# One more batch through the DMA crossbar, and one load issued beside the crossbar transposes (RWKV time mixing, 16 x 2048 x 256)

## The chip, the cores and the metric

One core of a Trainium2 chip runs the whole problem. The metric is the device time of one execution in microseconds, the median of several runs; three runs of the kernel before gave 198.86 to 199.21, median 199.1. A profile of one execution gives, for every engine, when each instruction ran and what it waited for.

The engines are TensorE (PE, matrix products and its own transposes), VectorE (DVE), ScalarE (ACT), GpSimd (POOL) and SyncE (SP, which here only issues DMAs). Sixteen DMA engines move data between HBM and the on-chip memory SBUF; they serve a queue q1 (issued by SP: stores and crossbar transposes) and a queue q0 (issued by POOL: loads that turn float32 into bfloat16 on the way).

## The reference

```python
x_prev = np.zeros_like(x)
x_prev[:, 1:, :] = x[:, :-1, :].copy()
xk = x * time_mix_k + x_prev * (1 - time_mix_k)
xv = x * time_mix_v + x_prev * (1 - time_mix_v)
xr = x * time_mix_r + x_prev * (1 - time_mix_r)
k = xk.reshape(-1, d_model) @ key_weight
v = xv.reshape(-1, d_model) @ value_weight
r = xr.reshape(-1, d_model) @ receptance_weight
r_sigmoid = 1.0 / (1.0 + np.exp(-r))
wkv = v
out = (r_sigmoid * wkv).reshape(-1, d_model) @ output_weight
```

x is 16 batches of 2048 tokens of 256 channels, float32. The result depends on r and v only; k isn't used. So per token: mix it with the token before in two ways, two products with 256 x 256 matrices, a sigmoid, an elementwise product, and one more product.

## The kernel before, in words

**Units.** The tokens are worked through in 64 units of 512, four to a batch; the main loop runs over the unit number g. Channels must lie on the partitions for the products, so each batch is needed transposed (`xt`). For a unit, TensorE makes the r product (`psum_r`, four matmuls), the v product (`psum_v`, four) and the output product of an earlier unit (`psum_o`, eight small ones). ACT makes the sigmoid `s_sb` and copies the output to `o_sb`; DVE multiplies `s_sb` with `psum_v` into `z_sb`. The mixed input `mix` is made ahead of the unit in two steps: one half of the channels is scaled on POOL (`scale_pool`, line 364), the other on DVE (`scale`, 354) or ACT (`scale_act`, 638), and then DVE adds the shifted tokens (`add`, 376). From unit 10 on the scalings are made once for a pair of units, for r (m = 0) in one unit and for v (m = 1) in the next, and from `FREE` on the one for v on ACT.

**Two ways to transpose.** Batches 0 to 9 are loaded into SBUF tiles `x_bf` and transposed on TensorE (`transposes`, line 272: eight 128 x 128 transposes in a unit, for the unit six ahead), and ACT copies the result out of PSUM (289). Batches from `STAGED` = 10 on are loaded as bfloat16 into a DRAM tile `x_natural` instead, and one DMA from SP (`by_dma`, line 254) reads it through the crossbar, transposed, into `xt_both`: batches 10 to 12 in one instruction issued in unit 27, 13 to 15 in another in unit 39 (`T_AT`). Each waits until the last load of its group has landed (`after`); the loads of batches 12 and 15 are in two halves (`HALVED`). A few rows of zeros stand ahead of each batch in DRAM (`zero_rows`, one small DMA in each unit from 12 on), which give the token before the first.

**What sets the order.** The order of every engine's instructions is the program's order, and each engine and each queue takes its instructions one after another. POOL issues the loads between its scalings. Loads 13, 14 and 15 are issued in units 33, 34 and 35 (`STAGE_AT`), and a dependency (`tc.add_manual_dep`) makes each wait until the crossbar transpose before them (`last_t`) has landed. SP issues the stores and the crossbar transposes: ahead of a transpose, stores that are held back until the first half of the last load has landed (`FIRST`), then the transpose, then the stores that were kept meanwhile (`WAITING`). A store is for a pair of units and named by its second one; store 19 is that of units 18 and 19.

**Tiles for the output.** Seven `o_sb` tiles go round; from the pair number `SPARE` on, four of each eleven are taken from the `x_bf` tiles that no load needs any more.

Of the kernel before, what the change touches and what calls it, by code (L numbers as in the profile page):

```python
# [9 lines left out]
BF16 = mybir.dt.bfloat16  # L10
# [5 lines left out]
def kernel(  # L16
# [27 lines left out]
    B, S, D = x.shape  # L44
    P = 128
    KO = D // P
    J = S // P
    UJ = 4
    TU = UJ * P
    UB = J // UJ  # L50
# [2 lines left out]
    BYUNIT = 2  # L53
    LONG = 2
    H = UJ // 2
    STAGED = 10
    BYDMA = NU - STAGED * UB
    CROSS = NU - BYDMA - LOOK
    FREE = CROSS
    LATE_O = CROSS - 2  # L60
    T_AT = {27: 10, 39: 13}
    FIRST = {19: 27, 21: 27, 27: 39}
    WAITING = {23: 27, 25: 27, 29: 39, 31: 39, 33: 39, 35: 39}
    ZEROS_AT = 12
    SINGLE = NU - 6
    STAGED_PAIRS = range(STAGED, B - 1)
    STAGE_AT = {33: 13, 34: 14, 35: 15}
    GROUPS = [(2, 3), (4, 5, 6), (7, 8, 9), (10, 11, 12), (13, 14, 15)]
    HALVED = (12, 15)
    PAD = 16  # L70
    SPARE = 9 * UB // 2
    NX, NO = 4, 7
    START_T = [1, 3, 5, 6, 7, 9, 11, 12]
    AHEAD = 6
# [7 lines left out]
        (2, 0): (5,),  # L82
        (3, 0): (6,),
        (4, 0): (7,),
        (5, 0): (8, 10),
        (6, 0): (9,),
        (7, 0): (11,),
        (7, 1): (12,),
    }

    consts = ctx.enter_context(tc.tile_pool(name="consts", bufs=1))
    xpool = ctx.enter_context(tc.tile_pool(name="xpool", bufs=NX))
    dpool = ctx.enter_context(tc.tile_pool(name="dpool", bufs=2, space=bass.MemoryType.DRAM))
    xtpool = ctx.enter_context(tc.tile_pool(name="xtpool", bufs=2))
    mixpool = ctx.enter_context(tc.tile_pool(name="mixpool", bufs=3))
    zpool = ctx.enter_context(tc.tile_pool(name="zpool", bufs=3))
# [15 lines left out]
    loads = {}  # L112
    xt_both = {}
    xt = {}
# [32 lines left out]
    def load(b):  # L147
        if b < STAGED:
            x_bf[b] = xpool.tile([P, J, D], BF16, name="x_bf")
# [41 lines left out]
    for e in (2, 3):  # L191
        op = nc.gpsimd.dma_start(out=x_first[:, e - 2], in_=unit_rows(x, 0, e)[:, 0])  # L192
# [17 lines left out]
    def new_xt(b):  # L210
        if b >= BYUNIT:
            for group in GROUPS:
                if b != group[0]:
                    continue
                if b >= STAGED:
                    t = xtpool.tile([P, KO, len(group) * (PAD + S)], BF16, name="xt_both")
                    for k in range(len(group)):
                        xt[b + k] = t[:, :, k * (PAD + S) + PAD - 1 : (k + 1) * (PAD + S)]
                    xt_both[b] = t
                    return  # L220
                xt_both[b] = xtpool.tile([P, J + 1, KO, len(group), P], BF16, name="xt_both")
                for k in range(len(group)):
                    xt[b + k] = xt_both[b][:, :, :, k]
                    nc.gpsimd.memset(xt[b + k][:, 0, :, 0:1], 0.0)
            return
        xt[b] = consts.tile([P, UB * (UJ + 1), KO, P], BF16, name=f"xt_first{b}")
        (nc.vector if b == 0 else nc.gpsimd).memset(xt[b][:, 0, :, 0:1], 0.0)

    new_xt(0)
# [21 lines left out]
    def by_dma(b, after):  # L251

        new_xt(b)
        op = nc.sync.dma_start_transpose(
            out=xt_both[b], in_=x_both[b].rearrange("b s d -> (b s) d")
        )
        tc.add_manual_dep(op.ins, after.ins.name, SYNC, reason="not beside a load")
        return op
# [66 lines left out]
    def tokens(piece, off, ko=None):  # L325

        b, _, lo, hi = piece
        if b in STAGED_PAIRS:
# [3 lines left out]
            return cols if ko is None else cols[:, ko]  # L332
        if b < STAGED:
            cols = xt[b][:, slots(piece, off)]
# [227 lines left out]

    pads = [p for group in GROUPS if group[0] >= STAGED for p in new_staged(group)]
    tnext = 1
# [57 lines left out]
    for u in range(2, NU):  # L622
# [3 lines left out]
        for m, (b, _, lo, hi) in enumerate(pieces(u)):  # L626
            w = first[u][m]
            group = (b, m, lo, hi + TU if paired else hi)
# [17 lines left out]
    for g in range(NU - 1):  # L646
        ps_r = ps_r_pool.tile([P, KO, TU], FP32, name="psum_r")
        if g == 0:
            project_unmixed(ps_r, 0)
            advance(1)  # L650
            project_unmixed(ps_r, 1)
            wrap_slots(pieces(1)[0])
            scale(pieces(1)[0])
            last = add(pieces(1)[0])
        else:
            project(ps_r, g, 0)
        s_sb = zpool.tile([P, KO, TU], BF16, name="s_sb")
        nc.scalar.activation(out=s_sb, in_=ps_r, func=ACT.Sigmoid)  # L658
        advance(START_T[g] if g < len(START_T) else g + LOOK)
        if g in T_AT:  # L660
            half, whole = loads[T_AT[g] + 2]
            for pair in firsts.pop(g):
                store(nc.sync, *pair, after=half)
            last_t = by_dma(T_AT[g], whole)
            for pair in kept.pop(g, []):
                store(nc.sync, *pair)
        if LATE_O < g < NU - 2:
            output(g - 2, z_prev2)
        for p in products.get(g + 1, []):
            if g >= FREE and p[0][1] == 1:  # L670
                scale_act(p[0], (0,))
        for p in [q for q, _ in products[g]] + pooled[g]:
            last_unit_of = p[3] // TU - 1
            need = last_unit_of if p[0] < BYUNIT else min(last_unit_of + 1, UB - 1)
            assert UB * p[0] + need < tnext, (g, p, tnext)
            if g > AHEAD or p not in pooled[g]:
                wrap_slots(p)
        if g == 1:
            load(2)
            scale_act(pieces(2)[1], (1,))  # L680
        for p, kos in products[g]:
            if not (g - 1 >= FREE and p[1] == 1):
                scale(p, kos)
        for p in sums[g]:
            last = add(p)
        for p in pooled[g]:
            if p[0] >= BYUNIT:
                wrap_slots(p)
        ps_v = ps_v_pool.tile([P, KO, TU], FP32, name="psum_v")
        project(ps_v, g, 1)  # L690
        if g == 0:
            scale_act(pieces(1)[1], (0,))
            advance(2)
        z_sb = zpool.tile([P, KO, TU], BF16, name="z_sb")
        n = TU // 2 if g == NU - 2 else TU
        for c in range(0, TU, n):
            nc.vector.tensor_tensor(  # L697
                out=z_sb[:, :, c : c + n],
                in0=s_sb[:, :, c : c + n],
                in1=ps_v[:, :, c : c + n],  # L700
                op=ALU.mult,
            )
        for p in pooled[g]:
            wrap_slots(p, after=last)
            scale_pool(p, last)
        if ZEROS_AT <= g < ZEROS_AT + len(pads):
            zero_rows(*pads[g - ZEROS_AT])
        if g in STAGE_AT:
            b = STAGE_AT[g]
            loads[b] = load(b)  # L710
            for op in loads[b] if b in HALVED else [loads[b]]:
                tc.add_manual_dep(op.ins, last_t.ins.name, SYNC, reason="not beside transposes")
        for p in held[g]:
            add(p)
        if z_prev is not None and not LATE_O <= g < NU - 3:
            output(g - 1, z_prev)
        z_prev2, z_prev = z_prev, z_sb
# [31 lines left out]
```

## Time and profile before

| what | value |
|---|---|
| median of three runs | 199.1 us (198.86 to 199.21) |
| span of the profiled execution, first to last instruction | 197.1 us |
| the profiled execution's own time | the page gives its span only; the median of the runs is 2.0 above it |
| busy: PE / DVE / ACT / POOL | 97% / 93% / 90% / 44% |
| DMA queues q1 / q0, share of 16 engines | 60.3% / 41.6% |
| a unit with TensorE transposes / without | about 3.05 / 2.60 us |
| issue of the two crossbar transposes | 95.4 and 133.9 us |

In the rows, `L272` is line 272 of the kernel, `x32` a count, and times are in us unless said. `PE psum_r L384` is the r product, `psum_v L384` the v product, `psum_o L416` the output product, `ps_t L272` a TensorE transpose. In the rows by window the columns are the stretch and its length, busy time and instructions of PE, weight loads, DVE, ACT and POOL, the granted TensorE clock, the busy share of the DMA engines and GB/s. A row of a DMA queue gives packets, MB and the share of the time of 16 engines that the packets took; shares above 100% mean that packets of one engine overlap.

### The profile page before, as it was taken

What the parts mean: (1) busy time and instruction counts of PE and PEld (TensorE: products, weight loads), DVE (VectorE), ACT (ScalarE), POOL (GpSimd) and SP (SyncE); (2) the same over time, 40 slices, a digit from 0 to 9 for tenths busy, and PEclk for the clock granted to TensorE, in tenths of its full rate; (3) what the DMA queues carried; (4) which work ended last, traced back from release to release, by engine and by line L of the source; (5) the groups of instructions that cost most, each with busy time, mean ns of one, the idle gap of its engine ahead of it and who ended that gap; (6) DMA issues with size and microseconds to landing.
All of it is one profiled execution on the core that took longest, in us unless ns stands there. A gap on an engine that the chain in (4) does not pass through costs nothing.

```text
span 197.1 us, 3735 instructions
## 1 busy us (share of the span) xinstructions
PE 191.5 (97%) x1358; PEld 123.0 (62%) x1364; DVE 183.1 (93%) x286; ACT 177.1 (90%) x197; POOL 86.3 (44%) x117
## 2 busy tenths in 40 slices
PE   8999999999999999999999999999999999999992
PEld 3556676666666666666666666666666666666660
DVE  0999999999999999999999999999999999999962
ACT  3699899999999999999999999999999999999982
POOL 2845542443665635624334266444433444444200
PEclk9999999999999999999999999999999999999998
DMA  5999999999999999999999999999999999999985
GB/s 185 238 176 224 218 254 262 247 259 262 296 413 283 283 296 332 283 238 198 376 209 290 335 346 186 212 218 241 290 290 419 419 421 419 416 416 421 382 327 221
DMA packets 35593, 58.13 MB, mean 295 GB/s; under 512 B 26004, under 2 KB 27128, under 8 KB 30840
## 3 DMA queue, kind: packets, MB, share of 16 engines
q1 hardware_dynamic: 31792, 41.34, 60.3%
q0 software_dynamic: 3632, 16.44, 41.6%
q8 instruction: 10, 0.16, 0.3%
q10 hardware_dynamic: 152, 0.13, 0.2%
q14 instruction: 7, 0.06, 0.1%
HBM read 34.34 MB, written 39.90 MB: 377 GB/s over the span
## 4 chain that ended last, share of the span: by engine, by line
PE 90%; DMA 6%; POOL 1%; issue 0%; SPq 0%; ACT 0%
PE psum_r L384 27%; PE psum_v L384 27%; PE psum_o L416 27%; PE ps_t L272 8%; DMA x_bf<-in_x_dram 4%; DMA w_f<-n_receptance_weight_dram 2%; PE ps_t L416 1%; POOL x_bf L192 1%; SPq L174 0%; POOL wo_bf L195 0%; PE psum_v L416 0%; POOL x_bf L152 0%; PE ps_t L384 0%; PE psum_r L416 0%; ACT x_bf L446 0%
## 5 line engine op out<-in xcount | busy, mean ns | idle before, releaser
L364 POOL TENSOR_SCALAR mix<-xt_both,c_sb 128x1024 bf16<-128x1024 bf16 (+1 forms) x55 | 61.1, 1110 | 85.5 <-DVE mix L376 82.3
L697 DVE TENSOR_TENSOR z_sb<-s_sb,psum_v 128x1024 bf16<-128x1024 bf16 (+1 forms) x64 | 76.8, 1201 | 2.3 <-PE psum_v L384 1.1
L376 DVE TENSOR_TENSOR mix<-mix,xt_both 128x1024 bf16<-128x1024 bf16 x112 | 76.8, 696 | 1.4
L384 PEld LDWEIGHTS <-w_bf 128*128 128x128 bf16 x512 | 48.5, 98 | 39.2 <-DVE mix L376 0.8
L658 ACT ACTIVATE s_sb<-psum_r 128x1024 bf16<-128x1024 f32 x63 | 65.2, 1034 | 6.2 <-PE psum_r L384 6.0
L384 PE MATMUL psum_v<-mix,w_bf 128*128 128x512 bf16 (+1 forms) x252 | 64.8, 378 | 0.4 <-DVE mix L376 0.2
L384 PE MATMUL psum_r<-mix,w_bf 128*128 128x512 bf16 x250 | 64.6, 379 | 0.2
L416 PE MATMUL psum_o<-wo_bf,z_sb 128*128 128x256 bf16 x486 | 63.2, 273 | 0.0
L416 PEld LDWEIGHTS <-z_sb 128*128 128x128 bf16 x512 | 52.0, 103 | 17.9 <-DVE z_sb L510 0.7
L471 ACT COPY o_sb<-psum_o 128x1024 f32<-128x1024 f32 x50 | 51.2, 1023 | 5.0 <-PE psum_o L416 4.8
L289 ACT COPY xt_both<-ps_t 128x1024 bf16<-128x1024 bf16 x32 | 32.9, 1039 | 0.0
L272 PEld LDWEIGHTS <-x_bf 128*128 128x128 bf16 x304 | 19.8, 98 | 8.4 <-DMA x_bf<-in_x_dram 0.4
L272 PE MATMUL ps_t<-ident,x_bf 128*128 128x128 bf16 x304 | 22.7, 219 | 0.2 <-DMA x_bf<-in_x_dram 0.2
L354 DVE TENSOR_SCALAR mix<-xt_both,c_sb 128x1024 bf16<-128x1024 bf16 (+1 forms) x47 | 21.3, 463 | 0.0
L638 ACT ACTIVATE mix<-xt_both,c_sb 128x1024 bf16<-128x1024 bf16 x14 | 16.3, 1163 | 0.0
L376 DVE TENSOR_TENSOR mix<-mix,xt_first 128x1024 bf16<-128x1024 bf16 x15 | 10.5, 708 | 0.1
L471 ACT COPY x_bf<-psum_o 128x1024 f32<-128x1024 f32 x10 | 10.2, 1015 | 0.0
L354 DVE TENSOR_SCALAR mix<-xt_first,c_sb 128x512 bf16<-128x512 bf16 x22 | 6.6, 350 | 0.3 <-ACT xt_first L282 0.2
L289 ACT COPY xt_first<-ps_t 128x1024 bf16<-128x1024 bf16 x6 | 6.0, 1022 | 0.0
L557 POOL COPY xt_first<-xt_first 128x254 bf16<-128x254 bf16 x5 | 2.0, 392 | 7.2 <-DVE mix L376 7.2
L162 POOL DMA_DIRECT2D x_bf<-in_x_dram x8 | 4.7, 584 | 0.0
L364 POOL TENSOR_SCALAR mix<-xt_first,c_sb 128x512 bf16<-128x512 bf16 x6 | 4.1, 685 | 1.3 <-DVE mix L376 0.8
(68 smaller groups left out, 52.3 us busy)
## 6 DMA issues: line engine op xcount, KB each, us to landing
out_dram<-o_sb SPq DMA_DIRECT2D x25, 1024.0 KB, 12.1
x_bf<-in_x_dram POOLq DMA_DIRECT2D x8, 1024.0 KB, 15.8
x_natural<-in_x_dram POOLq DMA_DIRECT2D x4, 1024.0 KB, 11.8
out_dram<-x_bf SPq DMA_DIRECT2D x4, 1024.0 KB, 14.4
x_natural<-in_x_dram POOLq DMA_DIRECT2D x4, 512.0 KB, 12.7
out_dram<-x_bf SPq DMA_DIRECT2D x4, 512.0 KB, 4.7
x_bf<-in_x_dram POOLq DMA_DIRECT2D x6, 256.0 KB, 7.0
o_sb<-in_x_dram SPq DMA_DIRECT2D x4, 256.0 KB, 3.9
```

Source lines behind the costliest of these rows:

```text
L162: return nc.gpsimd.dma_start(out=x_bf[b], in_=rows(b), max_dma_last_dim=run)
L272: nc.tensor.transpose(out=ps[:, jj], in_=src[:, jj, ko * P : (ko + 1) * P], identity=idn)
L289: nc.scalar.copy(out=xt[b][:, j0 : j0 + UJ], in_=ps)
L354: nc.vector.tensor_scalar(out=mixed(piece, ko), in0=tokens(piece, 0, ko), scalar1=c_sb[:, m, ko : ko + 1], scalar2=None, op0=ALU.mult,)
L364: op = nc.gpsimd.tensor_scalar(out=mixed(piece, 1), in0=tokens(piece, 0, 1), scalar1=c_sb[:, m, 1:2], scalar2=1.0, op0=ALU.mult, op1=ALU.mult,
L376: return nc.vector.tensor_tensor(out=mixed(piece), in0=mixed(piece), in1=tokens(piece, 1), op=ALU.add)
L384: nc.tensor.matmul(out=ps[:, mo, :], lhsT=w_bf[:, m, ko, mo * P : (mo + 1) * P], rhs=mixed((b, m, e * TU + lo, e * TU + hi), ko), start=(k ...
L416: nc.tensor.matmul(out=ps[:, j, :], lhsT=slot[:, ko, j], rhs=wo_bf[:, ko, :], start=(ko == 0), stop=(ko == KO - 1),)
L471: nc.scalar.copy(out=o[:, j0 : j0 + UJ, :], in_=ps)
L638: nc.scalar.activation(out=mixed(piece, ko), in_=tokens(piece, 0, ko), func=ACT.Copy, scale=c_sb[:, m, ko : ko + 1],)
L658: nc.scalar.activation(out=s_sb, in_=ps_r, func=ACT.Sigmoid)
L697: nc.vector.tensor_tensor(out=z_sb[:, :, c : c + n], in0=s_sb[:, :, c : c + n], in1=ps_v[:, :, c : c + n], op=ALU.mult,)
```

## The change

Batch 9 goes by DRAM and the crossbar as well (`STAGED` = 9), as a group of its own, with its own crossbar instruction issued in unit 27 right ahead of that of batches 10 to 12; its transposed tile takes the place of batch 0's. The TensorE transposes end four units earlier, and what follows from their end (`FREE`, `LATE_O`, `SPARE`) moves with it. Load 9 is issued with load 8 and load 10 in the place that load 9 had. Load 13 is issued in unit 27 instead of 33 and no longer waits for the crossbar (`BESIDE`). Loads 14 and 15 stay in units 34 and 35 and still wait for `last_t`, which is the transpose of 10 to 12. Store 21 moves from ahead of the transposes to behind them.

```diff
-    STAGED = 10
+    STAGED = 9
-    T_AT = {27: 10, 39: 13}
-    FIRST = {19: 27, 21: 27, 27: 39}
-    WAITING = {23: 27, 25: 27, 29: 39, 31: 39, 33: 39, 35: 39}
+    T_AT = {27: (9, 10), 39: (13,)}
+    FIRST = {19: 27, 27: 39}
+    WAITING = {21: 27, 23: 27, 25: 27, 29: 39, 31: 39, 33: 39, 35: 39}
...
-    STAGE_AT = {33: 13, 34: 14, 35: 15}
-    GROUPS = [(2, 3), (4, 5, 6), (7, 8, 9), (10, 11, 12), (13, 14, 15)]
+    STAGE_AT = {27: 13, 34: 14, 35: 15}
+    BESIDE = (13,)
+    GROUPS = [(2, 3), (4, 5, 6), (7, 8), (9,), (10, 11, 12), (13, 14, 15)]
...
-    SPARE = 9 * UB // 2
+    SPARE = STAGED * UB // 2 - 2
...
-        (5, 0): (8, 10),
-        (6, 0): (9,),
+        (5, 0): (8, 9),
+        (6, 0): (10,),
...
-    dpool = ctx.enter_context(tc.tile_pool(name="dpool", bufs=2, space=bass.MemoryType.DRAM))
+    dpool = ctx.enter_context(tc.tile_pool(name="dpool", bufs=3, space=bass.MemoryType.DRAM))
+    firstpool = ctx.enter_context(tc.tile_pool(name="firstpool", bufs=1))
...
-                    t = xtpool.tile([P, KO, len(group) * (PAD + S)], BF16, name="xt_both")
+                    pool, name = (firstpool, "xt_first0") if len(group) == 1 else (xtpool, "xt_both")
+                    t = pool.tile([P, KO, len(group) * (PAD + S)], BF16, name=name)
...
-        xt[b] = consts.tile([P, UB * (UJ + 1), KO, P], BF16, name=f"xt_first{b}")
+        xt[b] = firstpool.tile([P, UB * (UJ + 1), KO, P], BF16, name=f"xt_first{b}")
...
-            half, whole = loads[T_AT[g] + 2]
+            half, whole = loads[T_AT[g][-1] + 2]
             for pair in firsts.pop(g):
                 store(nc.sync, *pair, after=half)
-            last_t = by_dma(T_AT[g], whole)
+            for b in T_AT[g]:
+                last_t = by_dma(b, whole)
...
-            for op in loads[b] if b in HALVED else [loads[b]]:
+            for op in () if b in BESIDE else loads[b] if b in HALVED else [loads[b]]:
                 tc.add_manual_dep(op.ins, last_t.ins.name, SYNC, reason="not beside transposes")
```

## The prediction

> **What bounds the kernel now.** I read the busy shares and DMA queues first, then the chain of waits, the windows, and the order of time of GpSimd (POOL), VectorE (DVE) and the SP queue around 95 to 125 us.
>
> ```profile
> span 197.1 us, 3735 instructions
> ...
> PE 191.5 (97%) x1358; PEld 123.0 (62%) x1364; DVE 183.1 (93%) x286; ACT 177.1 (90%) x197; POOL 86.3 (44%) x117
> ...
> q1 hardware_dynamic: 31792, 41.34, 60.3%
> q0 software_dynamic: 3632, 16.44, 41.6%
> ```
>
> TensorE is 97% busy, and the two DMA queues that matter (q1 the stores and crossbar transposes, q0 the loads) fill 60.3 + 41.6 = 101.9% of the 16 engines. So both are nearly full, and the chain says what a unit costs:
>
> ```profile
> 104.83 0.86 PE psum_r L384 x4
> 105.69 0.45 PE ps_t L272 x8
> ...
> 107.88 0.86 PE psum_r L384 x4
> ...
> 118.36 0.86 PE psum_r L384 x4
> ...
> 120.96 0.86 PE psum_r L384 x4
> ```
>
> Unit 31 starts at 104.83 and unit 32 at 107.88: 3.05 us with eight transposes in it (0.45). Units 36 and 37 start at 118.36 and 120.96: 2.60 us, without. A unit that loses its eight transposes is 3.05 - 2.60 = 0.45 shorter. (Unit numbers follow from counting back from the last unit, 63.)
>
> ```profile
> 160.00:165.00 5.00, 4.95 (x32) 3.22 (x32) 4.98 (x8) 4.59 (x6) 2.24 (x2) 1.00 1.01 419
> ```
>
> In the later stage PE (4.95 of 5) and DVE (4.98 of 5) are both full at a granted clock of 1.00, and the DMA engines too (share 1.01, 419 GB/s of stores). What is lost there once isn't caught up again.
>
> **The change, part by part.** *Removed:* batch 9's 32 TensorE transposes, done beside units 30 to 33: 4 x 0.45 = **1.8 us off the PE chain**. With them go four ACT copies and one DVE copy of the shifted column; two scalings of 0.46 us move from DVE to ACT because FREE falls from 34 to 30.
>
> ```profile
> L289 ACT COPY xt_both<-ps_t 128x1024 bf16<-128x1024 bf16 x32 | 32.9, 1039 | 0.0
> ...
> L354 DVE TENSOR_SCALAR mix<-xt_both,c_sb 128x1024 bf16<-128x1024 bf16 (+1 forms) x47 | 21.3, 463 | 0.0
> ...
> L638 ACT ACTIVATE mix<-xt_both,c_sb 128x1024 bf16<-128x1024 bf16 x14 | 16.3, 1163 | 0.0
> ...
> L142 POOL DMA_DIRECT2D x_natural<-zeros x6 | 3.3, 554 | 0.0
> ```
>
> ACT gives up 4 x 1.04 and takes 2 x 1.16, so it is relieved. Units 30 to 33 then look like units 34 and later, where DVE keeps PE's pace; I see nothing that withholds the 1.8. The seventh zero fill costs POOL 0.55 us at unit 18; POOL is busy 44% and it costs nothing there. Loads 9 and 10 change places on the queue with the same bytes, so load 12 should land when it does now. The output tiles keep their distance: two more sit in the old x tiles from unit 32 on, and a tile filled late is still reused only eleven tiles later; nothing.
>
> *Added to the DMA:* one crossbar batch, 2064 x 256 x 2 bytes = 1.057 MB.
>
> ```profile
> 138.00:148.00 10.00, 9.89 (x61) 6.24 (x62) 9.98 (x15) 9.18 (x10) 4.09 (x5) 1.00 1.27 290
> ```
> ```profile
> q0 software_dynamic: 352, 2.11, 102.4%
> ```
>
> Crossbar traffic alone runs at 290 GB/s (first row), so one batch is 1.057 / 0.290 = 3.64 us. From 120 to 130 us only loads ran: 2.11 MB landed, so one batch load (1.05 MB in bf16) takes 5.0 us of all engines. A store of 1.05 MB at 419 GB/s takes 2.5 us.
>
> *Moved:* load 13 to unit 27, without its wait for the crossbar.
>
> ```profile
> 95.09 1.12 POOL L364 TENSOR_SCALAR mix<-xt_both,c_sb 128x1024 bf16<-128x1024 bf16 x1 [2.12 <-DVE mix L376]
> 97.84 1.12 POOL L364 TENSOR_SCALAR mix<-xt_both,c_sb 128x1024 bf16<-128x1024 bf16 x1 [1.63 <-DVE mix L376]
> ```
> ```profile
> q0 software_dynamic: 12, 0.10, 55.6%
> ```
>
> It is issued at about 96.2, in a gap of 1.63 us on POOL, so the 0.56 us issue is free. Its packets come some 2 us later, near 98.3, beside the transposes: the second row is the load queue from 116.5 to 117.5 us, with the first 12 packets of the load that is issued at 114.71 now. Store 21 moves behind them: 2.5 us of traffic less ahead, on the same SP queue; store 19 stays ahead.
>
> *What then waits:* loads 14 and 15 still depend on the last crossbar transpose (of 10 to 12), and load 14 is still issued by POOL in unit 34. This is the step I count most carefully.
>
> ```profile
> 113.48 1.12 POOL L364 TENSOR_SCALAR mix<-xt_both,c_sb 128x1024 bf16<-128x1024 bf16 x1 [2.33 <-DVE mix L376]
> 114.71 0.56 POOL L162 DMA_DIRECT2D x_natural<-in_x_dram  x1
> 116.23 1.11 POOL L364 TENSOR_SCALAR mix<-xt_both,c_sb 128x1024 bf16<-128x1024 bf16 x1 [0.96 <-DVE mix L376]
> 117.30 0.55 POOL L162 DMA_DIRECT2D x_natural<-in_x_dram  x1
> 118.66 1.11 POOL L364 TENSOR_SCALAR mix<-xt_both,c_sb 128x1024 bf16<-128x1024 bf16 x1 [0.81 <-DVE mix L376]
> 119.72 1.10 POOL L158 DMA_DIRECT2D x_natural<-in_x_dram  x2
> 121.41 1.11 POOL L364 TENSOR_SCALAR mix<-xt_both,c_sb 128x1024 bf16<-128x1024 bf16 x1 [0.58 <-DVE mix L376]
> ```
> ```profile
> L162 POOLq EVENT_SEMAPHORE x9: 17/17/43, 17.6 to 114.2; - x9
> ```
> ```profile
> L254 SPq DMA_TRANSPOSE xt_both<-x_natural x2: 12865/14030/15195, 95.4 to 133.9; - x2
> ...
> DMA to landing us min/median/max: 15.7/17.3/18.8
> ```
>
> The first transpose was issued at 95.4 and landed 18.8 later, at 114.2; the last wait of the POOL queue for a load ends at just that time, and POOL's scaling ran to 114.6 anyway. So the wait stands in POOL's own stream and is free today by 0.4 us. After the change, POOL reaches load 14 when scaling 34 ends: 116.23 + 1.11 - 1.8 = 115.5. If the crossbar lands at T, later than that, POOL stands still, and behind it stand scaling 35, the two halves of load 15, and scaling 36: 0.1 + 0.56 + 1.06 + 1.10 + 1.12 + 0.1 = 4.05 us of POOL work until scaling 36 is done, at T + 4.05.
>
> ```profile
> 122.36 1.30 DVE L376 TENSOR_TENSOR mix<-mix,xt_both 128x1024 bf16<-128x1024 bf16 x2
> 123.66 1.22 DVE L697 TENSOR_TENSOR z_sb<-s_sb,psum_v 128x1024 bf16<-128x1024 bf16 x1
> ```
>
> DVE wants it in the second of these two adds, which starts some 0.6 in, at 122.97 today, 121.2 after. So DVE is late by T - 117.1; behind the add stands unit 37's product z, which frees psum_v for unit 38.
>
> ```profile
> 122.69 0.86 PE psum_v L384 x4
> ...
> 125.29 0.86 PE psum_v L384 x4
> ```
>
> z ends at 124.88, PE wants the bank at 125.29: 0.41 with the handover, of which 0.2 stays after the following, longer DVE unit. **PE's loss is T - 117.3, and the whole gain is gone at T = 119.1.**
>
> ```profile
> q0 software_dynamic: 180, 1.34, 80.3%
> q1 hardware_dynamic: 110, 0.75, 23.1%
> ```
>
> *T.* The transposes wait for load 12, so they start at 95.4 as now. The nearest row is the second transpose, which also had one store in front of it: 15.7 from issue to landing (of which 3 x 3.64 = 10.9 is traffic). 95.4 + 15.7 + 3.64 for batch 9 = 114.7 without the load. What load 13 adds is shown nowhere. Lower end 0: the crossbar leaves 419 - 290 = 129 GB/s unused. Upper end 5.0: by the records the engines are 127% busy with the crossbar alone, and where loads and stores overlap (the two rows above, 80 to 88 us) their shares only add up, to 103%. A crossbar that fills the engines' time with small packets is nearer to these two rows, so I take 5.0 less some 0.5 that the load finds in the slow start of the transposes: **T = 114.7 + 4.5 = 119.2**. The Trainium skill, "DMA: Bandwidth & Descriptors", "Queues, rings and completion order", says that each DMA engine takes turns between its queues packet by packet. No run here shows a load beside a transpose; by that rule the load's whole 5.0 would go on top, T = 119.7, and by the spare rate it would be 114.7. The first transpose's 18.8, less 2.5 for the missing store, would give 0.6 more; and a second transpose instruction may pay a start of its own. So T lies in 114.7 to 121.
>
> *Sum:* -1.8 + (119.2 - 117.3 = 1.9) = +0.1. The sum is made in the profiled span of 197.1; the page gives nothing of what lies around it, and the runs' median is 2.0 above, which I keep: 199.1 + 0.1 = **199.2**.
>
> *The end.* DMA gets 3.64 more to do. Today 95.4 to 133.9 holds 35.2 us of traffic (three crossbar batches 10.9, three loads 15.0, two stores behind the first transpose and most of two ahead, 9.3) in 38.5; after it is 38.8 (3.64 more), and with the load beside the start some 2 less idle: the second transposes start about 2.0 later, and the stores behind them too.
>
> ```profile
> 186.00:196.00 10.00, 7.35 (x52) 4.72 (x50) 5.61 (x10) 6.62 (x12) 0.00 (x0) 0.98 0.78 306
> ```
>
> The last 10 us hold 2.2 us of idle DMA, so this is covered, barely, when PE ends no earlier; with the full PE gain it would take about 0.2 of it back. Batch 13 itself is wanted by POOL at unit 49, some 2 us after it would land.
>
> ```profile
> 134.00:138.00 4.00, 4.00 (x27) 2.70 (x26) 3.98 (x7) 3.59 (x5) 2.13 (x2) 1.00 1.16 197
> ```
>
> **Rivals.** *The load finds room* (T up to 117.3): for it the 129 GB/s; against it the 127%. POOL's wait then ends before it matters: 199.1 - 1.8 + 0.2 (the end, above) = 197.5; with half of the load hidden (114.7 + 2.5 = 117.2) the same. *Slower: POOL's queue behind load 14.* The same wait decides, from T = 119.5 on (0.2% over): with the second instruction's start exposed (the row above: the first four us of the old second one move 197 of 290 GB/s, some 1.3 to 2 us lost) T = 121.0, PE loses 3.7, 199.1 - 1.8 + 3.7 = 201.0. For it: two instructions where one was; against it: the load can fill that gap. *The change isn't felt*: batch 9 lands late, and unit 36 waits as long as it gained, 199.1; against it, 95.4 + 15.7 - 2 x 3.64 + 5.0 = 108.8 is the latest for one batch, and POOL wants it at about 112.
>
> **How the numbers follow.** A difference of 0.2% (0.4 us) is about what a measurement can tell. Main case, T near 119.2 (118.5 to 120.5: 198.5 to 200.5): 0.45, of which 0.08 faster, 0.25 same, 0.12 slower. Room for the load: 0.32, faster. Long POOL wait: 0.18, slower. Not felt: 0.05, same. So faster 0.40, same 0.30, slower 0.30. The range is 197.4 (full gain, a little taken back by the end) to 201.0 (T = 121); the main case alone is 198.5 to 200.5.
>
> **What would show it.** Units 30 to 33 at 2.60 apart. The landing of the transpose of 10 to 12, near 119.2, as the end of POOL's wait ahead of load 14; POOL idle before it from 115.5, scaling 36 near 122.2, and a hole of about 1.9 us in PE's chain at unit 38. DMA share about 1 through the load. If the transpose lands by 117.3 there is no hole and I am wrong on the faster side; if after 120.5, on the slower.

## The result, and the profile after

The changed kernel takes 216.6 us in the median of four executions (211.4, 214.4, 218.7, 227.7); the kernel before takes 199.2 beside it (198.9 to 199.6). The ratio is 1.068, interval 1.062 to 1.074: slower, and far outside the predicted 197.4 to 201.0; the shortest execution is still 12 us longer than the kernel before. The ratio leaves out the two longest executions as disturbed, while the profile is of the one of 218.7, so the sizes read from it are those of a longer execution.

The page of the changed kernel, its span and engines, its two large queues, and the shares of the chain that ended last:

```profile
span 216.9 us, 3671 instructions
...
PE 192.8 (89%) x1324; PEld 122.1 (56%) x1332; DVE 183.4 (85%) x283; ACT 175.4 (81%) x195; POOL 87.7 (40%) x117
...
q1 hardware_dynamic: 35952, 42.40, 65.0%
q0 software_dynamic: 3664, 16.44, 39.2%
...
PE 71%; DMA 22%; POOL 1%; issue 1%; DVE 1%; SPq 0%; ACT 0%; POOLq 0%
```

TensorE was 97% busy and is 89% now. The chain was PE's alone around the first transposes; now 22% of it is DMA (6% before), and 18 of the 22 are two pieces (the chain in order of time: start, length, what):

```profile
95.48 17.55 DMA xt_first<-x_natural
113.03 21.51 DMA xt_both<-x_natural
```

The first is the crossbar of batch 9 as far as the issue of the second instruction; the second is that of batches 10 to 12, which lands at 113.03 + 21.51 = 134.5. The prediction had 119.2. SP's queue and then POOL in order of time (start, length, instruction, and in brackets the idle time before it and what ended it) show who stood still:

```profile
95.48 17.25 SPq L257 DMA_TRANSPOSE xt_first<-x_natural  x1
113.03 19.46 SPq L257 DMA_TRANSPOSE xt_both<-x_natural  x1
...
153.32 13.54 SPq L257 DMA_TRANSPOSE xt_both<-x_natural  x1
```
```profile
96.18 0.56 POOL L164 DMA_DIRECT2D x_natural<-in_x_dram  x1
...
122.58 2.93 POOL L367 TENSOR_SCALAR mix<-xt_first,c_sb 128x1024 bf16<-128x1024 bf16 x2 [12.22 <-DMA xt_first<-x_natural]
135.07 0.55 POOL L164 DMA_DIRECT2D x_natural<-in_x_dram  x1 [9.56 <-DMA xt_both<-x_natural]
```

Load 13 is issued at 96.2, as forecast. POOL then stands 12.22 us for batch 9 and 9.56 us, ahead of load 14, for batches 10 to 12. The windows (stretch, length, busy time and instructions of PE, weight loads, DVE, ACT and POOL, granted clock, DMA share, GB/s) price it:

```profile
112.00:140.00 28.00, 13.03 (x66) 6.78 (x65) 11.78 (x15) 9.67 (x10) 6.90 (x8) 0.78 1.22 220
```
```profile
104.00:108.00 4.00, 4.00 (x29) 2.54 (x27) 4.00 (x5) 3.55 (x4) 2.24 (x2) 1.00 0.93 140
...
116.00:120.00 4.00, 0.00 (x0) 0.00 (x0) 0.00 (x0) 0.00 (x0) 0.00 (x0) 1.00 1.51 49
120.00:124.00 4.00, 0.00 (x0) 0.00 (x0) 1.57 (x3) 1.51 (x2) 1.42 (x1) 0.61 1.08 199
124.00:128.00 4.00, 3.08 (x9) 1.17 (x10) 3.98 (x5) 1.44 (x2) 1.51 (x2) 0.54 1.27 194
...
136.00:140.00 4.00, 1.84 (x5) 0.74 (x6) 2.17 (x3) 0.00 (x0) 3.08 (x5) 0.50 1.07 391
140.00:144.00 4.00, 4.00 (x25) 2.63 (x23) 4.00 (x6) 3.38 (x4) 2.22 (x2) 0.83 1.01 256
...
206.00:216.00 10.00, 3.66 (x27) 2.19 (x25) 2.25 (x5) 3.43 (x7) 0.00 (x0) 0.85 0.81 313
```

Between 112 and 140 PE is idle 28 - 13.03 = 15.0 us, and the granted clock falls in the two holes and is still low when PE begins again: 3.08 us of work at 0.54, 1.84 at 0.50 and 4.00 at 0.83 are worth 1.4 + 0.9 + 0.7 = 3.0 us less at full clock. With the 1.8 won ahead of it, PE should end 15.0 + 3.0 - 1.8 = 16.2 later. It ends at 206 + 3.66 = 209.7, against 184 + 9.35 = 193.35 before (next row, of the kernel before), so 16.3 later. The other 3.5 us of the span's 19.8 are stores behind PE's end.

```profile
184.00:196.00 12.00, 9.35 (x66) 6.20 (x63) 7.61 (x12) 8.62 (x14) 0.90 (x1) 0.98 0.81 322
```

In the row from 116 to 120 every engine stands still, the DMA engines are called 151% busy, and they move 49 GB/s. That is the place to look. The queues of the changed kernel from 104 to 108 us, then from 100 to 121 (packets, MB, share of the time of 16 engines):

```profile
q0 software_dynamic: 65, 0.52, 71.5%
q1 hardware_dynamic: 171, 0.04, 21.7%
```
```profile
q1 hardware_dynamic: 1828, 0.47, 77.5%
q0 software_dynamic: 143, 1.04, 42.0%
```

The load of 1.04 MB takes the 21 us from 100 to 121, instead of 5.0, and the crossbar moves 0.47 MB in that time, which it moves in 1.6 us alone (0.47 / 0.290).

### The profile page after: what moved, and what is told of

It reads as the page before. It is cut to its first block, busy times and chain, and to the rows that moved or that the text cites. A ratio compares the mean times of both kernels' runs of the same rounds, so it can differ in the third digit from the quotient of the medians.

```text
span 216.9 us, 3671 instructions
## 1 busy us (share of the span) xinstructions
PE 192.8 (89%) x1324; PEld 122.1 (56%) x1332; DVE 183.4 (85%) x283; ACT 175.4 (81%) x195; POOL 87.7 (40%) x117
## 4 chain that ended last, share of the span: by engine, by line
PE 71%; DMA 22%; POOL 1%; issue 1%; DVE 1%; SPq 0%; ACT 0%; POOLq 0%
PE psum_r L387 21%; PE psum_o L419 21%; PE psum_v L387 21%; DMA xt_both<-x_natural 10%; DMA xt_first<-x_natural 8%; PE ps_t L275 6%; DMA x_bf<-in_x_dram 2%; DMA w_f<-n_receptance_weight_dram 2%; PE ps_t L419 1%; DVE mix L379 1%; POOL mix L367 1%; SPq L176 0%; POOL x_bf L194 0%; PE psum_v L419 0%; POOL x_natural L164 0%
## 5 line engine op out<-in xcount | busy, mean ns | idle before, releaser
L367 POOL TENSOR_SCALAR mix<-xt_both,c_sb 128x1024 bf16<-128x1024 bf16 (+1 forms) x51 | 56.6, 1110 | 78.6 <-DVE mix L379 72.4
L661 ACT ACTIVATE s_sb<-psum_r 128x1024 bf16<-128x1024 f32 x63 | 65.1, 1034 | 16.2 <-PE psum_r L387 15.9
L379 DVE TENSOR_TENSOR mix<-mix,xt_both 128x1024 bf16<-128x1024 bf16 x104 | 71.2, 696 | 1.1
L474 ACT COPY o_sb<-psum_o 128x1024 f32<-128x1024 f32 x46 | 47.1, 1025 | 4.1 <-PE psum_o L419 4.0
L292 ACT COPY xt_both<-ps_t 128x1024 bf16<-128x1024 bf16 x28 | 28.8, 1042 | 0.0
L379 DVE TENSOR_TENSOR mix<-mix,xt_first 128x1024 bf16<-128x1024 bf16 x23 | 17.5, 769 | 6.8 <-POOL mix L367 6.7
L275 PE MATMUL ps_t<-ident,x_bf 128*128 128x128 bf16 x272 | 20.1, 220 | 0.4 <-DMA x_bf<-in_x_dram 0.4
L641 ACT ACTIVATE mix<-xt_both,c_sb 128x1024 bf16<-128x1024 bf16 x14 | 16.3, 1162 | 0.0
L357 DVE TENSOR_SCALAR mix<-xt_first,c_sb 128x512 bf16<-128x512 bf16 (+1 forms) x24 | 7.4, 357 | 9.4 <-DMA xt_first<-x_natural 9.1
L367 POOL TENSOR_SCALAR mix<-xt_first,c_sb 128x512 bf16<-128x512 bf16 (+1 forms) x10 | 9.4, 945 | 13.0 <-DMA xt_first<-x_natural 12.2
L474 ACT COPY x_bf<-psum_o 128x1024 f32<-128x1024 f32 x14 | 14.2, 1013 | 0.5 <-PE psum_o L419 0.5
L641 ACT ACTIVATE mix<-xt_first,c_sb 128x512 bf16<-128x512 bf16 (+1 forms) x4 | 3.8, 943 | 8.3 <-DMA xt_first<-x_natural 8.3
L164 POOL DMA_DIRECT2D x_natural<-in_x_dram x5 | 2.9, 570 | 9.6 <-DMA xt_both<-x_natural 9.6
```

The lines of the kernel that those rows point to most:

```text
L164: return nc.gpsimd.dma_start(out=x_bf[b], in_=rows(b), max_dma_last_dim=run)
L275: nc.tensor.transpose(out=ps[:, jj], in_=src[:, jj, ko * P : (ko + 1) * P], identity=idn)
L292: nc.scalar.copy(out=xt[b][:, j0 : j0 + UJ], in_=ps)
L357: nc.vector.tensor_scalar(out=mixed(piece, ko), in0=tokens(piece, 0, ko), scalar1=c_sb[:, m, ko : ko + 1], scalar2=None, op0=ALU.mult,)
L367: op = nc.gpsimd.tensor_scalar(out=mixed(piece, 1), in0=tokens(piece, 0, 1), scalar1=c_sb[:, m, 1:2], scalar2=1.0, op0=ALU.mult, op1=ALU.mult,
L379: return nc.vector.tensor_tensor(out=mixed(piece), in0=mixed(piece), in1=tokens(piece, 1), op=ALU.add)
```

## The experiments

The twelve runs at a glance; "waits" is the change with load 13 waiting for the transposes. T is the landing of the transpose of batches 10 to 12, then the end of the issue of the second crossbar instruction (batches 13 to 15) and the span, of the profiled execution (a dash where the profile doesn't show it); the times are those of all executions, or their lowest and highest. Before has T = 114.2, 146.7, 197.1 and a time of 198.9 to 199.3 (its medians beside these runs).

| kernel | T | second crossbar's end | span | time, us |
|---|---|---|---|---|
| the change | 134.5 | 166.9 | 216.9 | 211.4 to 227.7 |
| batch 9 by crossbar, load 13 waits | 115.5 | 151.7 | 201.8 | 203.3 to 203.6 |
| before, load 13 beside | 118.6 | 147.2 | 198.3 | 200.1, 209.0 |
| the same again | 121.1 | 150.1 | 199.8 | 199.9, 201.6, 213.4, 213.6 |
| change, load 13 in small packets | 130.8 | 161.6 | 212.4 | 201.9, 214.2 |
| change, load 13 in unit 30 | 125.5 | 156.9 | 207.6 | 209.0, 209.4 |
| before, load into SBUF beside | 139.3 | 172.6 | 223.4 | 213.3 to 233.5 |
| before, store 23 beside | 119.2 | 151.5 | 202.1 | 203.9, 204.7 |
| waits, store 21 between the crossbars | 120.0 | 153.4 | 203.5 | 204.4 to 205.2 |
| waits, store 21 ahead | 118.5 | 152.6 | 202.6 | 203.1 to 204.5 |
| load 13 ahead of the crossbars | 122.3 | 153.4 | 203.4 | 204.0 to 206.3 |
| waits, three stores left out | 114.8 | 149.9 | 199.6 | 199.0 to 201.4 |
| before, three stores left out | - | 145.6 | 197.5 | 199.2 to 201.3 |

Wherever all stores are written, the span follows the second crossbar's end: 20.1 later and 19.8 longer with the change, 5.0 and 4.7 with the load waiting, 25.9 and 26.3 with the load into SBUF. In the two runs with load 13 beside and no fourth batch they part by up to 0.8, elsewhere by less than 0.5.

**The two halves of the change: batch 9 by the crossbar, load 13 waiting as before** (one unit later each for the three loads).

```diff
-    STAGE_AT = {27: 13, 34: 14, 35: 15}
-    BESIDE = (13,)
+    STAGE_AT = {34: 13, 35: 14, 36: 15}
+    BESIDE = ()
```

> Batch 9 by the crossbar as in the change, but load 13 waits for the crossbar again (loads 13, 14, 15 in units 34, 35, 36). Theory A (the load beside the crossbar is what costs): crossbar at 290 GB/s throughout, batch 9 lands near 104 us, batches 10 to 12 near 115.5, no long hole in PE; time 197.3 to 198.5. Rival B (a fourth batch or a second crossbar instruction is what costs): the crossbar lands after 120 us again and the time is above 201.

Measured: 203.3, ratio 1.022 (1.020 to 1.023), and the four executions lie within 0.3 us of each other. The landing is what theory A said, the time is not. SP's queue of this kernel:

```profile
95.81 5.08 SPq L257 DMA_TRANSPOSE xt_first<-x_natural  x1
101.19 12.23 SPq L257 DMA_TRANSPOSE xt_both<-x_natural  x1
...
139.44 12.30 SPq L257 DMA_TRANSPOSE xt_both<-x_natural  x1
```

Without the load the first two instructions take 5.08 and 12.23 us instead of 17.25 and 19.46; the transpose lands at 101.19 + 14.3 = 115.5. So the load beside the transposes is what adds 19.0 to T, and the wide spread of the times goes with it. PE's gain is there as well. The starts of the r products of units 28 and 36, in the chain of before and then of this kernel:

```profile
95.69 0.86 PE psum_r L384 x4
```
```profile
95.88 0.86 PE psum_r L387 x4
...
103.76 0.86 PE psum_r L387 x4
106.36 0.86 PE psum_r L387 x4
...
116.76 0.43 PE psum_r L387 x2
```

Eight units take 118.36 - 95.69 = 22.67 before and 116.76 - 95.88 = 20.88 here: 1.79 less, with 2.60 from unit to unit. Yet the kernel is 4.4 slower than before. Its windows say why:

```profile
102.00:104.00 2.00, 2.00 (x14) 1.24 (x13) 2.00 (x4) 1.99 (x3) 0.60 (x1) 1.00 1.04 175
104.00:106.00 2.00, 2.00 (x15) 1.29 (x14) 2.00 (x4) 2.00 (x3) 1.12 (x1) 1.00 1.29 201
...
184.00:196.00 12.00, 8.27 (x57) 5.23 (x54) 6.56 (x11) 7.54 (x13) 0.00 (x0) 0.93 1.01 411
196.00:200.00 4.00, 0.00 (x0) 0.00 (x0) 0.00 (x0) 0.00 (x0) 0.00 (x0) 0.50 0.74 269
```

PE ends at 184 + 8.27 = 192.3, 1.1 earlier than before, and the DMA engines, full to 196, still move stores till about 200: the end is theirs. The start of the second instruction loses (290 - 175 + 290 - 201) x 2 / 290 = 1.4 us of crossbar, and 3.64 + 1.4 = 5.0 is what the second crossbar's end is late by (151.74 - 146.73). That the 1.4 belongs in this sum is argued from the windows and not shown: no run makes the four batches one instruction, and the run below that puts a store into the start of the first instruction wins nothing.

**Is the end really the DMA engines'? Three stores taken out**, of units 20 to 25 (numbers 21, 23 and 25, whose output rows are not written), 7.5 us of traffic, from the kernel above and from before:

```diff
-            if g in FIRST:
+            if g in (21, 23, 25):
+                pass
+            elif g in FIRST:
```

> Batch 9 by the crossbar and load 13 waiting, as in e1, but the three stores 21, 23 and 25 (3 MB of the output, units 20 to 25) are left out, 7.5 us of DMA time. Theory D (e1 ends late because the DMA engines have more work than time, not because an engine waits): the last stores land 2 us after their issue again and the end is TensorE's, 197.0 to 198.0. Rival E (e1 lost its time in waits of PE, DVE or POOL): 202 to 203.5.

> The kernel before without the same three stores (the output of units 20 to 25 is not written). The kernel before is bound by TensorE's chain, so both theories expect no change, 198.6 to 199.2; if it falls by more than 0.5, the DMA was holding the kernel before too. The distance from here to f1 is what four units without TensorE transposes are worth when the DMA has room: 1.8 by the sum, 0 by rival E.

Measured: 199.2 with batch 9 by the crossbar (4.1 less than with its stores; ratio to before 1.002, 0.999 to 1.006), and 199.8 from before (1.004, 1.001 to 1.007). The kernel before gains nothing by leaving them out, the one with the fourth batch 4.1: its end is set by DMA traffic, as theory D said. But neither time fell into its expected range: 199.2 is above D's 197.0 to 198.0, and the first kernel comes out 0.5 below the second, not 1.8. The last windows, of the first (an execution of 201.4, the longest of its ten) and then of the second:

```profile
184.00:196.00 12.00, 7.58 (x53) 4.91 (x51) 5.84 (x10) 6.84 (x12) 0.00 (x0) 0.89 1.02 406
```
```profile
184.00:196.00 12.00, 9.18 (x65) 6.08 (x63) 7.44 (x12) 8.45 (x14) 0.73 (x1) 0.97 0.72 285
```

PE ends 9.18 - 7.58 = 1.6 earlier with batch 9 by the crossbar, but even with 7.5 us less to store its DMA engines are full (1.02) where those of before have 28% free. The gain on PE is real, but little of it reaches the time.

**Load 13 beside, without the fourth batch**, two runs of one kernel:

```diff
-    STAGE_AT = {33: 13, 34: 14, 35: 15}
+    STAGE_AT = {27: 13, 34: 14, 35: 15}
...
-            for op in loads[b] if b in HALVED else [loads[b]]:
+            for op in () if b == 13 else loads[b] if b in HALVED else [loads[b]]:
```

> The kernel before with one edit: load 13 in unit 27 without its wait; batch 9 stays on TensorE, one crossbar instruction. Theory A: the crossbar falls below 100 GB/s while the load is under way and lands at 125 to 132 us instead of 114; POOL stands at load 14 until then, and the time is 205 to 212. Rival B: the load adds its 5 us at most, the crossbar lands by 119, time 199 to 201.

> The kernel of e2 again (kernel before, load 13 beside the one crossbar instruction), for the spread of its times, since two executions gave 200.05 and 209.01. If two modes exist (the crossbar pauses for the load and goes on, or both trickle), times fall near 200 and near 205 to 212, and the profiled execution shows which; if one of the two was an accident of that run, all four lie within 1 us.

Measured: 200.1 and 209.0; again 199.9, 201.6, 213.4 and 213.6. Two clusters, nothing between 202 and 209. Both profiles fell into the lower one. SP's queue of the first, and its queues from 104 to 108 and from 108 to 112:

```profile
95.03 21.60 SPq L254 DMA_TRANSPOSE xt_both<-x_natural  x1
```
```profile
q0 software_dynamic: 97, 0.66, 79.5%
q1 hardware_dynamic: 490, 0.13, 15.9%
...
q1 hardware_dynamic: 4459, 1.14, 127.7%
```

Here the load goes through and the crossbar waits: 0.13 MB in four us, then 1.14 at its full rate. T is 118.6, 4.4 later than before and near the load's 5.0: the sum that I had in mind, and rival B's. In the second run T is 121.1. The change's profile shows another way for the same two transfers to meet. Times of 209.0 to 213.6 would fit that way, which was theory A's, but no profile shows one of these executions.

**Small packets for load 13**, so that the crossbar might get its turn more often:

```diff
-        run = 8192 if b < LONG else 16384
+        run = 8192 if b < LONG else 2048 if b in BESIDE else 16384
```

> The changed kernel with load 13 cut into runs of 2048 bytes of float32 instead of 16384. Theory A1 (a crossbar step waits in all engines for the longest packet that one of them has in hand, 0.62 us for 8 KB): with packets an eighth as long the waits shrink, batch 9 lands by 110 and batches 10 to 12 by 122; time 199 to 203. Rival A2 (each change between the queues costs a fixed time of about a microsecond, whatever the packet): eight times the packets, the crossbar is later than in the changed kernel, time above 220.

Measured: 201.9 and 214.2; in the latter T is 130.8. SP's second instruction there:

```profile
107.56 21.19 SPq L257 DMA_TRANSPOSE xt_both<-x_natural  x1
```

Smaller packets don't cure it: T is still 15 us later than with the load waiting. Nor do they make it worse, so rival A2 (over 220 us) falls. The execution of 201.9 is in theory A1's range, but with two executions it shows no more than that the spread is still there.

**Load 13 three units later**, into a crossbar that is already running:

```diff
-    STAGE_AT = {27: 13, 34: 14, 35: 15}
+    STAGE_AT = {30: 13, 34: 14, 35: 15}
```

> The changed kernel with load 13 issued in unit 30 (about 104 us), when batch 9 has landed and the crossbar of batches 10 to 12 runs at full rate. Theory A (any packets of another queue hold the crossbar up, at any time): batch 9 lands by 105 and unit 36 does not wait for it, but batches 10 to 12 land at 120 to 135; time 203 to 212. Rival S (the collapse needs the load at the start of a crossbar instruction, or two of them): 10 to 12 land by 118 and the time is that of e1, 203, or less.

Measured: 209.2, ratio 1.051 (1.049 to 1.054), two executions 0.4 apart. Batch 9 lands in time, and T is 125.5, as theory A said. The queues from 112 to 116, and POOL's wait:

```profile
q0 software_dynamic: 50, 0.39, 53.1%
q1 hardware_dynamic: 130, 0.03, 11.0%
```
```profile
126.03 0.56 POOL L164 DMA_DIRECT2D x_natural<-in_x_dram  x1 [10.56 <-DMA xt_both<-x_natural]
```

The crossbar breaks down from full flow just as it does at its start: 0.03 MB in 4 us, where it had moved 1.16. So it doesn't take the start of a transpose.

**Is it the load's writes into DRAM?** The crossbar reads DRAM, load 13 writes it. So the kernel before with one more load in unit 27, into an unused tile of SBUF, that nothing reads:

```diff
+        if g == 27:
+            scratch = xpool.tile([P, J, D], BF16, name="x_bf")
+            nc.gpsimd.dma_start(out=scratch, in_=rows(13), max_dma_last_dim=16384)
```

> The kernel before, with one load added in unit 27 beside the first crossbar transpose: the same rows of batch 13 from the same queue, with the same packets, but into an unused tile of SBUF and not into the DRAM scratch (nothing reads it; everything else, load 13 at its old place too, is unchanged). Theory (the crossbar stops for the packets of any other queue, as it did for a store into DRAM from ACT's queue): the crossbar of 10 to 12 lands 4.5 to 7 later than 114.2 in a good execution and 10 or more in a bad one, POOL waits for it ahead of load 13, and the time is 201 to 215, spread over more than 2. Rival (reads of the crossbar and writes of the load meet in DRAM, so a load into SBUF does little): it lands by 117.5, and the time is 199 to 201.5, spread under 1. The load's own 5.0 us of DMA work is extra in both.

Measured: 213.3 to 233.5, the slowest of all. SP's queue, POOL's wait, and the queues from 104 to 108:

```profile
95.59 41.56 SPq L254 DMA_TRANSPOSE xt_both<-x_natural  x1
```
```profile
139.77 0.56 POOL L162 DMA_DIRECT2D x_natural<-in_x_dram  x1 [24.44 <-DMA xt_both<-x_natural]
```
```profile
q1 hardware_dynamic: 60, 0.02, 64.8%
q0 software_dynamic: 15, 0.12, 14.6%
```

Writes into DRAM are not needed for it, so that rival falls; the theory's own range for a bad execution ("10 or more", up to 215) was too small, since T is 25 late. The last two rows show the breakdown at its worst. In 4 us of 16 engines, 64 engine-us, 60 crossbar packets took 64 x 0.648 / 60 = 0.69 us each, and 15 load packets 64 x 0.146 / 15 = 0.62. Alone, a crossbar packet takes 64 x 1.277 / 4459 = 0.018 us (the last row quoted for load 13 beside without the fourth batch). So in this window a crossbar packet of 256 bytes lasts as long as a packet of the load, and the load has only 15 packets in 4 us, where it alone has 352 in 10 (the row quoted in the prediction). Both queues are nearly still. In the change it was less extreme: from 104 to 108 a crossbar packet took 64 x 0.217 / 171 = 0.08 us.

**A store beside, and not a load**: store 23 from ACT's queue in unit 30, in the kernel before.

```diff
+    beside = []
...
+            elif g == 23:
+                beside.append(pair)
...
+        if g == 30:
+            store(nc.scalar, *beside.pop())
```

> The kernel before with store 23 taken off SP's queue and issued from ACT in unit 30, in the middle of the first crossbar transpose: a hardware queue, 1 MB, no conversion. Theory A (any packet of another queue holds the crossbar up): the crossbar falls below 150 GB/s while the store is under way and lands after 118 instead of 114. Rival C (only the software queue's loads, or their conversion, do it): the store adds its 2.5 us at most, landing by 117, and the time is 199 to 200.

Measured: 204.3, ratio 1.027 (1.023 to 1.030). The queues from 108 to 112 (q10 is ACT's), and POOL:

```profile
q10 hardware_dynamic: 96, 0.78, 46.0%
q1 hardware_dynamic: 148, 0.04, 7.5%
```
```profile
119.66 0.56 POOL L163 DMA_DIRECT2D x_natural<-in_x_dram  x1 [5.13 <-DMA xt_both<-x_natural]
```

The crossbar stands nearly still (0.04 MB in 4 us) while the store's 0.78 MB pass, and T is 5.0 later for 2.5 us of traffic. So a load on the software queue is not needed to stop the crossbar. But here the stop is short, with no trickle.

**The same amount on SP's own queue**: the kernel with the waiting load, store 21 between the two crossbar instructions.

```diff
+                if b == 9:
+                    store(nc.sync, *kept[27].pop(0))
```

> Like the kernel with batch 9 by crossbar and load 13 waiting (203.3), but store 21 stands on SP's own queue between the crossbar of batch 9 and that of 10 to 12, so its packets come in turn on the queue that the crossbar itself uses. Theory (only packets of another queue stop the crossbar): no stand-still; batch 9 lands where it did, 10 to 12 land later by the store's own 2.5 us, near 118.0 instead of 115.5; POOL waits some 2.5 ahead of load 13; time within 1 us of 203.3. Rival (any other packet beside the crossbar stops it, and a store cost 5 on ACT's queue): 10 to 12 land at 120.5 or later and the time is 204.5 or more.

Measured: 205.1, ratio 1.027 (1.020 to 1.034), T = 120.0. The theory missed: it had 118.0 and at most 204.3. The rival had 120.5 or later and 204.5 or more, so its time came out and its landing not quite. From 108 to 116 us the crossbar runs at its 290 GB/s, so nothing trickles; but T is 4.5 later than with store 21 behind both, 0.5 of it from a later start, so 2.5 us of store cost about 4 on the crossbar's own queue, against 5.0 on another one. For a store, the queue makes little difference.

**Can the order be mended?** Store 21 ahead of the transposes again, with the load waiting; then load 13 right behind load 12, ahead of both transposes, which wait for it:

```diff
-    FIRST = {19: 27, 27: 39}
-    WAITING = {21: 27, 23: 27, 25: 27, 29: 39, 31: 39, 33: 39, 35: 39}
+    FIRST = {19: 27, 21: 27, 27: 39}
+    WAITING = {23: 27, 25: 27, 29: 39, 31: 39, 33: 39, 35: 39}
```

> Batch 9 by crossbar and load 13 waiting as before (203.3 with store 21 behind the transposes), but store 21 ahead of them, as the kernel before has it. Theory: of the 5.0 by which the second crossbar's issue ended later (151.74 against 146.73), 3.64 is the batch itself and the rest is DMA time that stands empty while the two first transposes start; the store fills some of it, so the issue ends near 150.5 and the time is 202.0 to 202.8, still 3 above before. Rival (the moved store is what costs): the issue ends by 149 and the time is 199 to 200.5. Rival (no matter where the store is): 203.0 to 203.6.

```diff
-    STAGE_AT = {27: 13, 34: 14, 35: 15}
-    BESIDE = (13,)
+    STAGE_AT = {36: 14, 37: 15}
+    BESIDE = ()
...
-        (7, 1): (12,),
+        (7, 1): (12, 13),
...
+            if g == 27:
+                whole = loads[13]
```

> The change with load 13 ahead of the transposes and not beside: issued right behind load 12, both first transposes wait for it, loads 14 and 15 wait for them in units 36 and 37. Theory (the order on the DMA engines decides, and the end of the second crossbar sets the end): load 13 lands near 100.5, five behind load 12; batch 9 lands near 105.6, 10 to 12 near 120.5, no stand-still; loads 14 and 15 need 10.5 more and the second crossbar's issue ends near 145 to 147, as before (146.7). Time 197.5 to 200, so no more than 1 us from before, since PE's 1.6 is won only if the DMA engines lose nothing. Rival (the fourth crossbar batch by itself costs 4, wherever the load is): 202 to 204.

Measured: 204.0 (ratio 1.022, 1.015 to 1.029) and 205.5 (1.030, 1.022 to 1.037). SP's queue of the first, then of the second:

```profile
138.97 13.59 SPq L257 DMA_TRANSPOSE xt_both<-x_natural  x1
```
```profile
103.37 3.78 SPq L257 DMA_TRANSPOSE xt_first<-x_natural  x1
...
140.73 12.68 SPq L257 DMA_TRANSPOSE xt_both<-x_natural  x1
```

Neither theory held. With the store ahead the second crossbar ends at 152.6 and not at 150.5: filling the first instruction's start with a store won nothing, and the time is nearest to the rival by which the store's place doesn't matter (203.0 to 203.6). With the load ahead the transposes start at 103.4, not at 100.5, since stores run beside the two loads; the crossbars run clean, but the second one ends at 153.4 and not by 147. That is the rival's side, though 205.5 is above its 202 to 204: the fourth batch costs four to six us wherever load and store stand. No version here beats the kernel before.

## Why the prediction was wrong, step by step

**Removed, 1.8 us of PE.** Right: 1.79 between units 28 and 36, and 1.6 at PE's end in the runs without the three stores. "I see nothing that withholds the 1.8" was right for that stage and wrong for the kernel, by the end (below).

**One crossbar batch, 3.64 us at 290 GB/s, and T = 114.7 without the load.** Nearly right: with the load waiting, T is 115.5, and 0.4 of the 0.8 more is a later start of the first instruction (95.81 against 95.4). The second instruction's start I had priced (1.3 to 2 us) for the long POOL wait alone; by the windows it is 1.4, which T does not show in full.

**"What load 13 adds is shown nowhere. Lower end 0 ... Upper end 5.0."** This is the step that failed. It added 134.5 - 115.5 = 19.0 in the profiled execution. The shorter executions of the change, 211.4 and 214.4, have no profile; in the run with load 13 in unit 30 it added 125.5 - 115.5 = 10.0, twice the upper end. The lower end came from the crossbar's rate when it runs alone, the upper end from rows of loads and stores whose shares add up; no row had another transfer beside the crossbar. The Trainium skill, "DMA: Bandwidth & Descriptors", "Queues, rings and completion order", has the engines take turns packet by packet, and I worked out from it that the load's whole 5.0 would go on top. In the two profiles in which the load passes, T is 4.4 and 6.9 later and that sum is near; in the change, with the load into SBUF and in unit 30 it is too small by up to 20 us, and there the measurement decides. Taking turns is no promise that both keep their rates: a crossbar packet, 0.018 us alone, took 0.08 in one window of the change and 0.69 in one beside the load into SBUF.

**"108.8 is the latest for one batch, and POOL wants it at about 112."** Wrong by the same step: batch 9 was there at 122.5, and POOL lost 12.2 us on it. I had seen the mechanism (the rival in which batch 9 lands late), but gave it 0.05 and a price of 1.8, since the 5.0 was its upper end.

**POOL's wait ahead of load 14.** Right in kind: 9.56 us of idle POOL with scalings and load 15 behind it. The threshold of 117.3 fits the runs with the fourth batch, roughly. With the load waiting T = 115.5 is under 117.3, and the units of that kernel from 103.76 on are 2.60 apart, with no hole. With store 21 ahead the transpose lands at 118.5 and POOL starts its load at 119.0, so the rule gives a loss of 1.2 to 1.7; PE lost 0.65 + 1.10 = 1.75 there (the rows below). In the kernel before with load 13 beside, where POOL comes to load 14 about 1.8 later, the same rule gives no loss at T = 118.6, yet PE worked only 3.11 us from 120 to 124; so the wait can cost earlier than I worked out.

```profile
120.00:124.00 4.00, 3.35 (x22) 1.95 (x20) 2.52 (x4) 2.79 (x4) 3.96 (x6) 1.00 1.04 248
124.00:128.00 4.00, 2.90 (x17) 1.67 (x17) 4.00 (x6) 3.30 (x5) 2.25 (x2) 1.00 0.95 197
```

**"The end ... this is covered, barely."** Wrong, and it alone would have missed: with T at 115.5 and the full gain on PE, the time is still 203.3. I had the second transposes 2.0 later; their issue starts 139.44 - 133.86 = 5.6 later and ends 5.0 later. The 2.2 us of idle DMA in the last 10 us were used (a share of 1.01 from 184 to 196 with the load waiting, 0.81 before), but they are less than half of the 5.0. And the last traffic thins out for longer: the share stays near 1 until 198.5, 3.3 us ahead of the end, and in the kernel before until 195.5, 1.6 us ahead of it; 5.0 - 2.2 + 1.7 = 4.5 is about the 4.7 by which the span grew. And "if PE ends no earlier" was the wrong condition to lean on: a kernel in which DMA ends last gets nothing from PE. My opening reading, queues at 101.9% and both nearly full, had the answer: it should have been a rival of its own, the fourth batch as a net loss, worked out from the DMA total.

**The range.** Its upper end rested on the upper end of 5.0. An operation pair that no row of the trace showed was given bounds by rows of another kind, and the profiled execution has nearly four times that upper end.

**What stays open.** Why the load passes in some executions and trickles for 20 us and more in others; the two profiles with the lower times show the first, the change and the load into SBUF the second. While both are under way the numbers of their packets are of the same order: 171 of the crossbar and 65 of the load from 104 to 108 in the change, 73 and 55 in the second run with load 13 beside. With 256 bytes in one kind and 8 KB in the other, that would make the crossbar stand while the load passes, but it doesn't explain why the load slows as well. That crossbar packets hold a place on the engines while they wait for others would fit the 0.69 us, but it is argued and not shown.

## What to carry to other kernels

Don't put a load or a store beside crossbar transposes on the strength of free bandwidth: measure the pair, since here a load of 5.0 us delayed the transposes by anything from 4 to 25. When two resources are both near 100%, work moved from one to the other has to be priced at the end of both; here 1.8 us won on PE cost 5.0 on DMA engines that had 2.2 to spare. A wait that someone has written into a kernel ("not beside transposes") deserves an experiment of its own before it is taken out.

## What the runs showed of the hardware

A load or a store of 1 MB beside a crossbar transpose did not share the engines with it in any run here: at best the transpose nearly stood still (0.04 MB in 4 us beside the store), at worst both did (0.02 and 0.12 MB in 4 us beside the load into SBUF), with executions of one and the same kernel up to 20 us apart. The records call the engines busy all the while (93% to 151% in the windows of the change), so a full DMA share is no sign of traffic; GB/s beside it is.

The granted clock fell during a hole in PE's work and came back only after PE had begun again. In the change it stood at 1.00 in the first 4 us without work, at 0.61 in the next 4 and at 0.54 in those in which PE began again; after the second hole it was 0.50, and 0.83 in the four us after that. With load 13 in unit 30 it was 0.57 from 124 to 128, without work, and 0.50 from 128 to 132, with PE at work again. In the change this cost 3.0 us on top of 15.0 of idle time.
